# A merge's small products, their turning and its parts placed later among projections, and the last output half in a bank of its own

## The chip, the cores and the metric

The kernel runs on one core of one Trainium2 chip. The metric is the device time of one launch in microseconds (us), lower is better. Besides the plain runs there is one execution of the kernel before that the hardware profiler recorded, and all rows below are from it. The engines are named as the profile names them: PE is TensorE (matmul), DVE is VectorE, ACT is ScalarE, POOL is GpSimd, SP is SyncE, which issues most of the DMAs.

## The reference

One layer of a diffusion backbone on 1024 latent tokens (16 rows of 64) and 256 context tokens, model width 1024, all in fp32:

```python
# x: (1, 1024, 1024); modulated by adaLN, then one input projection for both branches
q, k, v, gate  = 8 heads of 64      # neighbourhood attention, window 8 x 16, plus all context keys
q, k, v, gate  = 4 heads of 128     # gated delta rule, chunks of 64, both directions
t_inv = triangular_solve(eye + a, eye)        # a: 64 x 64, strictly lower, one per chunk and direction
u = t_inv @ (v * beta);  w = t_inv @ (kb * exp(gc))
# scan over chunks from the context's final state
y = concat(attention * silu(gate), delta * silu(gate)) @ w_out
out = x + gate_ada * rmsnorm(y)
```

## The kernel before

Each fp32 product is made of three matmuls on split operands (hh·wh, hl·wh, hh·wl: a high and a low half). The program is written as Python generators; a scheduler orders the instructions of each engine from the program order, priorities and modelled times, and each engine then works through its own queue in that order.

The stage that the change touches is `phase_a2`. On PE it runs the projections for attention, pair of heads by pair (`self.fill`): the tiles pq, pk, pz of 512 columns (queries, keys and gate; pz2_0 and pz2_1 are the two 512-token halves of pair 2's gate), 24 matmuls each on 128x512. They accumulate in PSUM banks of one tag with three buffers ("pj"), so that a tile's first matmul waits until the tile three back has been read. `qk_out` reads a query or key tile twice: ACT copies out the high half (sh_), DVE subtracts to get the low half (sl_), both are stored to DRAM by SP. The sh_, sl_ and gate (st_z) tiles share four buffers.

Beside the projections two other generators are advanced by credits, per step of the fill 4 for `blocks()` and 1.5 for `merges()`. `blocks()` inverts the 32x32 diagonal blocks of the last group on DVE, some sixty short steps (ab_vv and tb_qh, L1255 and L1258, 80 partitions and 31 to 256 elements). `merges()` builds each head's 64x64 and 128-wide inverses out of these blocks, by `inv_merge`, which has parts in this order for a head h:

- l: load pmf (the products' other operand) and vl (the inverted blocks, four loads);
- t: on DVE three 32x32-wise transposes, vx from vl, vd from vx, ld from vd (lines 1291 to 1293), and ACT copies into tm;
- z: on PE the 32x32 products tz (two PSUM tiles of 20 products x 2), ACT copies them to zt, and ACT and POOL copy into xo and tm;
- u: on PE the 32x32 products tu, DVE copies them into tm and xo;
- w: on PE 64x64 products (tz2h_..., 20 of them), ACT copies them to z2;
- e: on PE 64x64 products (tu2h_...), DVE copies into tm, and SP stores tm to tm_dram.

tm is built in tm0 or tm1 (by the head's parity) and in tm2, which all heads share. The table MERGES ("0l 0t 1l 0z 1t 0u 0w 2l ...") gives the order in which the heads' parts are handed out, one by one.

Behind `phase_a2` come attention (scores sc from the loads kk, qh, ql) together with the delta scan, and last the output projection, whose tiles py are 512 columns wide. The last of them, (7, 1), is written in two halves of 256 columns, LAST = 256, one after the other into the same PSUM bank; `out_tile` then reads each half by ACT (sum of squares into ysq) and DVE (product with ggb).

## Time and profile before

| what | value |
|---|---|
| median of 3 runs | 851.81 us (849.72 to 855.88) |
| the profiled execution's own time | 848.82 us |
| its span | 847.1 us |
| PE busy | 814.2 us, 96% |
| DVE, ACT, POOL busy | 495.0, 418.0, 365.5 us |
| mean granted PE clock | 0.99 |
| longest PE wait | 5.58 us, head 0's first tz product, at 453.32 |

Between the profiled execution's time and its span lie 1.7 us. A busy share is an average over stages; what a stage waits for stands in its own rows. In a timeline row the first number is the start in us from the span's start, the second the length, and a bracket at the end holds the engine's idle time before the instruction and what ended it.

### The profile page before, as it was taken

The numbers are of one execution on the slowest core, as the hardware profiler recorded it, in microseconds if no ns is written. First come the engines' busy times: TensorE is split into PE (matmuls) and PEld (weight loads), VectorE is DVE, ScalarE is ACT, GpSimd is POOL, SyncE is SP. The second block draws the span as 40 slices with busy tenths as digits, with TensorE's granted clock in tenths as the row PEclk, the third lists the DMA queues.
The fourth block names the chain that finished last, engine by engine and source line by source line (L and its number), as shares of the span: only waits on it lengthen the run. The fifth ranks groups of instructions, "written<-read, shape, count | busy, mean of one in ns | idle before, by whom it ended". The sixth has DMA issues, their size and how long they took to land.

```text
span 847.1 us, 16613 instructions
## 1 busy us (share of the span) xinstructions
PE 814.2 (96%) x6170; PEld 695.3 (82%) x6170; DVE 495.0 (58%) x988; ACT 418.0 (49%) x1097; POOL 365.5 (43%) x436
## 2 busy tenths in 40 slices
PE   8999999999999999988997999899999999999996
PEld 6688887888788878878985787799898989878885
DVE  4673455546456757699926955556566565743342
ACT  4472525654564664643214334566666666753211
POOL 0042221363482572555452103565757567835121
PEclk9999999999999999999998999999999999999999
DMA  9986442254626626733688579996967923234261
GB/s 332 341 305 213 136 138 90 79 180 161 162 75 227 197 69 230 218 110 102 202 241 239 166 223 293 392 306 181 313 186 257 250 97 128 87 125 137 99 199 50
DMA packets 86343, 159.67 MB, mean 188 GB/s; under 512 B 18405, under 2 KB 45750, under 8 KB 84086
## 3 DMA queue, kind: packets, MB, share of 16 engines
q1 hardware_dynamic: 78774, 144.94, 54.0%
q10 hardware_dynamic: 7488, 13.67, 5.5%
q8 instruction: 49, 0.80, 0.4%
q14 instruction: 32, 0.26, 0.1%
HBM read 109.51 MB, written 52.42 MB: 191 GB/s over the span
## 4 chain that ended last, share of the span: by engine, by line
PE 76%; DMA 9%; DVE 7%; POOL 3%; issue 2%; ACT 2%; SPq 0%; DVEq 0%; POOLq 0%; ACTq 0%
PE py L1550 4%; PE py L1552 3%; PE py L1551 3%; PE pz L607 3%; PE pz L608 3%; PE pz L603 3%; PE pa L1437 3%; DMA vl<-yd 2%; PE po L942 2%; PE po L937 2%; PE tr L926 2%; PE sc L905 2%; PE pa L1422 2%; PE pv L618 2%; PE pv L617 2%; PE pv L616 2%
## 5 line engine op out<-in xcount | busy, mean ns | idle before, releaser
L909 DVE CUSTOM_DVE_ANT_0 pt<-sc,gm 128x544 f32<-128x544 f32 (+1 forms) x64 | 49.4, 772 | 32.3 <-PE sc L905 28.6
L910 ACT ACTIVATE pt<-pt,nm 128x544 f32<-128x544 f32 (+1 forms) x64 | 50.5, 789 | 31.1 <-DVE nm L909 30.7
L893 POOL TENSOR_TENSOR gm<-gt,mk 128x288 f32<-128x288 f32 (+1 forms) x48 | 46.5, 972 | 21.8 <-DVE nm L909 18.6
L1412 POOL TENSOR_SCALAR kd<-kt,kd 128x128 f32<-128x128 f32 x72 | 42.7, 604 | 18.7 <-PE pa L1451 18.2
L1040 DVE SCALAR_TENSOR_TENSOR acc_v<-xp_v,cols,acc_v 128x1282 f32<-128x1282 f32 x16 | 33.1, 2068 | 26.9 <-ACT acc_v L1038 26.6
L1193 POOL TENSOR_SCALAR_AFFINE_SELECT qe<-qe 128x256 f32<-128x256 f32 x32 | 29.0, 907 | 39.8 <-DVE qe L1192 39.8
L1616 DVE TENSOR_TENSOR finv<-py,ggb 128x512 f32<-128x512 f32 (+1 forms) x17 | 10.7, 656 | 51.4 <-ACT finv L1615 43.0
L603 PE MATMUL pz<-hh,wh_gz 128*128 128x512 f32 x96 | 38.9, 405 | 0.0
L607 PE MATMUL pz<-hl,wh_gz 128*128 128x512 f32 x96 | 38.8, 405 | 0.0
L608 PE MATMUL pz<-hh,wl_gz 128*128 128x512 f32 x96 | 38.8, 404 | 0.0
L1174 ACT ACTIVATE em<-em,gc 128x128 f32<-128x128 f32 x80 | 25.5, 390 | 25.7 <-DMA em<-gc_dram 22.9
L618 PE MATMUL pv<-wl_nv,hh 128*128 128x264 f32 x104 | 30.5, 296 | 4.8 <-DVE wl_nv L586 4.8
L1189 DVE SCALAR_TENSOR_TENSOR pm<-pk,nsc,em 128x128 f32<-128x128 f32 x80 | 23.5, 342 | 18.5 <-PE pk L1182 14.6
L1418 POOL TENSOR_SCALAR vb<-v,beta 128x128 f32<-128x128 f32 x40 | 24.2, 606 | 23.0 <-DVE y L1424 13.1
L586 POOL TENSOR_TENSOR wl_gz<-wr_gz,wh_gz 128x512 fp32r<-128x512 f32 x12 | 15.5, 1290 | 37.3 <-ACT wh_gz L585 35.8
L926 PE MATMUL tr<-c,pt 128*96 128x128 f32 (+1 forms) x192 | 31.4, 273 | 0.0
L1454 DVE SCALAR_TENSOR_TENSOR s<-s,egl,pa 128x128 f32<-128x128 f32 x64 | 19.4, 342 | 20.1 <-PE pa L1451 20.1
L924 ACT COPY tcx<-tc 128x256 f32<-128x256 f32 x64 | 23.5, 367 | 15.1 <-PE tc L919 14.5
L928 ACT COPY tl<-tr 96x384 f32<-96x384 f32 (+1 forms) x64 | 30.5, 476 | 0.0
L617 PE MATMUL pv<-wh_nv,hl 128*128 128x264 f32 x104 | 30.0, 291 | 0.0
L616 PE MATMUL pv<-wh_nv,hh 128*128 128x264 f32 x104 | 29.2, 292 | 0.0
L1615 ACT ACTIVATE finv<-py 128x512 f32<-128x512 f32 x14 | 8.3, 598 | 38.7 <-PE py L1552 20.5
(469 smaller groups left out, 2859.3 us busy)
## 6 DMA issues: line engine op xcount, KB each, us to landing
wada<-in_w_ada SPq DMA_DIRECT2D x16, 512.0 KB
em<-gc_dram SPq DMA_DIRECT2D x20, 256.0 KB
pm_dram<-pm SPq DMA_DIRECT2D x20, 256.0 KB
tm_dram<-tm SPq DMA_DIRECT2D x8, 640.0 KB
kk<-qk_dram SPq DMA_DIRECT2D x16, 320.0 KB
tm<-tm_dram SPq DMA_DIRECT2D x4, 1280.0 KB
kq_dram<-kq SPq DMA_DIRECT2D x4, 1152.0 KB
kq<-kq_dram SPq DMA_DIRECT2D x4, 1152.0 KB
```

The source lines that it names most:

```text
L603: r = nc.tensor.matmul(ps, wh, xh, start=(k == 0 and first), stop=False)
L607: nc.tensor.matmul(ps, wh, xl, start=False, stop=False)
L608: nc.tensor.matmul(ps, wl, xh, start=False, stop=(k == KC - 1))
L616: nc.tensor.matmul(ps, xh, wh, start=(k == 0), stop=False)
L617: nc.tensor.matmul(ps, xl, wh, start=False, stop=False)
L618: nc.tensor.matmul(ps, xh, wl, start=False, stop=(k == KC - 1))
L893: r = nc.gpsimd.tensor_tensor(self.gm[hh][:, 384 - n:384].rearrange("p (n c r) -> p n c r", c=nco, r=4), gv, self.mk[:, mo:mo + n].rearran ...
L909: nc.vector.tensor_tensor_reduce(pt[:, 384 - n:], sc[:, 512 - n:768], gm[:, 384 - n:], -1.0, 3.0e38, ALU.add, ALU.min, nm)
L910: self.last_exp = nc.scalar.activation(pt[:, 384 - n:], pt[:, 384 - n:], AF.Exp, bias=nm, scale=-1.0, accum_out=sums[:, ct, hh:hh + 1]).in ...
L926: self.pe(nc.tensor.transpose(pl[:m, rc * P:(rc + 1) * P], pt[:, 384 + (rc - 3) * m:384 + (rc - 2) * m], self.ident))
L1412: r = nc.gpsimd.tensor_scalar(kd[d], kt_[:, t, :], self.kd[:, h, d, t:t + 1], None, ALU.mult)
L1550: nc.tensor.matmul(py, mh[:, tt], wh[:, nn], start=(k == W_ORDER[0]), stop=False)
```

## The change

Three things are edited. `mm_chan` keeps the names of the last matmuls of its groups of three and `qk_out` that of the DVE instruction of the low half; with them, head 0's first transpose is ordered behind the last low half on DVE, and head 0's first tz product behind the last matmul recorded by then on PE (`order` sets an order on a queue, no semaphore). `merges()` holds head 0's part t until four steps of the fill are done and its part z until six, and its credit per step is 1.5 up to the sixth step and 2 from there. The second half of the last output tile gets a PSUM tile of its own, py7_2, and `out_tile` takes the halves from a list.

```diff
     def mm_chan(...):
-            nc.tensor.matmul(ps, wl, xh, start=False, stop=(k == KC - 1))
+            self.chans.append(nc.tensor.matmul(ps, wl, xh, start=False, stop=(k == KC - 1)).ins.name)
...
     def qk_out(...):
         if i:
-            nc.vector.tensor_tensor(kv(lo, "c r"), kv(src, "r c"), kv(hi, "c r").bitcast(F32), ALU.subtract)
+            r = nc.vector.tensor_tensor(kv(lo, "c r"), kv(src, "r c"), kv(hi, "c r").bitcast(F32), ALU.subtract)
         else:
-            nc.vector.scalar_tensor_tensor(lo, src, scale, hi.bitcast(F32), ALU.mult, ALU.subtract)
+            r = nc.vector.scalar_tensor_tensor(lo, src, scale, hi.bitcast(F32), ALU.mult, ALU.subtract)
+        self.low = r.ins.name
...
     def inv_merge(...):
-        nc.vector.transpose(vx, vl)
+        r = nc.vector.transpose(vx, vl)
+        if h == 0:
+            self.order(r, self.low)
...
-                    nc.tensor.matmul(pz[s2, t, :], pm[d][s1, t, s2], ld[s1, d, t, :], start=True, stop=True,
-                                     tile_position=(32 * b, 32 * b + 32))
+                    r = nc.tensor.matmul(pz[s2, t, :], pm[d][s1, t, s2], ld[s1, d, t, :], start=True, stop=True,
+                                         tile_position=(32 * b, 32 * b + 32))
+                    if h == d == t == b == 0:
+                        self.order(r, self.chans[-1])
...
     # output projection
-                for c0 in range(0, 512, LAST if tn == (7, 1) else 512):
-                    products(pys[tn], *tn, rest, c0, LAST if tn == (7, 1) else 512)
+                parts = [pys[tn]]
+                if tn == (7, 1):
+                    parts.append(ps.tile([P, 1024], F32, name="py7_2", tag="sc", bufs=1)[:, :512])
+                for i, py in enumerate(parts):
+                    products(py, *tn, rest, LAST * i, 512 // len(parts))
...
     def out_tile(...):
-            src = py[nn.start // 512][:, nn.start % 512:(nn.stop - 1) % 512 + 1]
+            src = py[i][:, nn.start % 512:(nn.stop - 1) % 512 + 1]
...
     def merges(parts):
+                while c == "0t" and steps < 4 or c == "0z" and steps < 6:
+                    yield
...
-        for _ in self.fill:
-            for i, r in enumerate((4, 1.5)):
+        for steps, _ in enumerate(self.fill, 1):
+            for i, r in enumerate((4, 1.5 if steps < 6 else 2)):
```

The lines of the rows below are moved by 1 to 5 in the changed kernel. First PE, in the middle of pair 2's gate, before: tz0_0 and tz0_1 are head 0's tz products.

```order
L603 MATMUL pz2_0_4738<-hh_115,wh_gz2_4_4733 128x512
L1305 MATMUL tz0_0_4491<-ld0_4338,pmf0_0_4330 32x32 [waits DMAHW4_49,DVE_49]
L1305 MATMUL tz0_0_4491<-ld0_4338,pmf0_0_4330 32x32 x19
L1305 MATMUL tz0_1_4514<-ld0_4338,pmf0_1_4332 32x32 [waits DMAHW5_49]
L1305 MATMUL tz0_1_4514<-ld0_4338,pmf0_1_4332 32x32 x19
L607 MATMUL pz2_0_4738<-hl_116,wh_gz2_4_4733 128x512
L608 MATMUL pz2_0_4738<-hh_115,wl_gz2_4_4734 128x512
L603 MATMUL pz2_0_4738<-hh_115,wh_gz2_4_4733 128x512
L607 MATMUL pz2_0_4738<-hl_116,wh_gz2_4_4733 128x512
L608 MATMUL pz2_0_4738<-hh_115,wl_gz2_4_4734 128x512
L603 MATMUL pz2_1_4797<-hh_115,wh_gz2_0_4727 128x512 [waits DVE_49]
```

The same engine in the changed kernel, the passage from pz2_0 to pz2_1, and then the end of pz2_1:

```order
L603 MATMUL pz2_0_4568<-hh_115,wh_gz2_4_4563 128x512
L607 MATMUL pz2_0_4568<-hl_116,wh_gz2_4_4563 128x512
L608 MATMUL pz2_0_4568<-hh_115,wl_gz2_4_4564 128x512
L603 MATMUL pz2_1_4660<-hh_115,wh_gz2_0_4557 128x512 [waits DVE_49]
L607 MATMUL pz2_1_4660<-hl_116,wh_gz2_0_4557 128x512
```

```order
L607 MATMUL pz2_1_4660<-hl_116,wh_gz2_4_4563 128x512
L1308 MATMUL tz0_0_4598<-ld0_4338,pmf0_0_4330 32x32 [waits DMAHW4_49,DVE_49]
L1308 MATMUL tz0_0_4598<-ld0_4338,pmf0_0_4330 32x32 x19
L1308 MATMUL tz0_1_4621<-ld0_4338,pmf0_1_4332 32x32 [waits DMAHW5_49]
L1308 MATMUL tz0_1_4621<-ld0_4338,pmf0_1_4332 32x32 x19
L608 MATMUL pz2_1_4660<-hh_115,wl_gz2_4_4564 128x512
```

The tz0 products moved from behind the nineteenth product of pz2_0 to ahead of the last one of pz2_1; the first product of pz2_1, with its wait on DVE, now comes ahead of them.

Second DVE at the same time, before: vx0, vd0, ld0 are head 0's transposes, sl_k20 is the low half of pair 2's first key tile.

```order
L1255 TENSOR_TENSOR tb2_qh0_4311<-ab_vv_4309 80x87 [waits DVE_49]
L1291 STREAM_TRANSPOSE vx0_4352<-vl0_4334 128x1024 [waits DMAHW5_49,DMAHW6_49,DMAHW4_49,DMAHW7_49,DMAHW1_49,DMAHW0_49]
L1258 TENSOR_TENSOR ab_vv_4309<-ab_vv_4309,tb2_qh0_4311 80x29x3 [waits DVE_49]
L1292 STREAM_TRANSPOSE vd0_4337<-vx0_4352 128x640 [waits DVE_49]
L1255 TENSOR_TENSOR tb2_qh0_4311<-ab_vv_4309 80x112 [waits DVE_49]
L1293 STREAM_TRANSPOSE ld0_4338<-vd0_4337 128x640 [waits DVE_49]
L1258 TENSOR_TENSOR ab_vv_4309<-ab_vv_4309,tb2_qh0_4311 80x28x4 [waits DVE_49]
L1255 TENSOR_TENSOR tb2_qh0_4311<-ab_vv_4309 80x135 [waits DVE_49]
L1291 STREAM_TRANSPOSE vx1_4545<-vl1_4335 128x1024 [waits DMAHW6_49,DMAHW7_49,DMAHW5_49,DMAHW4_49]
L1258 TENSOR_TENSOR ab_vv_4309<-ab_vv_4309,tb2_qh0_4311 80x27x5 [waits DVE_49]
L677 TENSOR_TENSOR sl_k20_4579<-pk2_0_4553,sh_k20_4578 128x512 [waits DMAHW0_49,Activation_49]
```

And in the changed kernel:

```order
L1256 TENSOR_TENSOR tb2_qh0_4311<-ab_vv_4309 80x207 [waits DVE_49]
L677 TENSOR_TENSOR sl_k20_4498<-pk2_0_4472,sh_k20_4497 128x512 [waits DMAHW0_49,Activation_49]
L1292 STREAM_TRANSPOSE vx0_4507<-vl0_4334 128x1024 [waits DMAHW6_49,DMAHW5_49,DMAHW7_49,DMAHW4_49,DMAHW1_49]
L1259 TENSOR_TENSOR ab_vv_4309<-ab_vv_4309,tb2_qh0_4311 80x23x9 [waits DVE_49]
L677 TENSOR_TENSOR sl_k21_4541<-pk2_1_4515,sh_k21_4540 128x512 [waits DMAHW2_49,Activation_49]
L1295 STREAM_TRANSPOSE vd0_4337<-vx0_4507 128x640 [waits DVE_49]
L1256 TENSOR_TENSOR tb2_qh0_4311<-ab_vv_4309 80x220 [waits DVE_49]
L1296 STREAM_TRANSPOSE ld0_4338<-vd0_4337 128x640 [waits DVE_49]
```

The transposes of head 0 moved behind sl_k20, and the steps of the inversion up to 207 elements moved ahead of both. SP's queue is the same in this place, from the loads of vl1 over the store of sl_q21 up to the store of sh_k20.

Third SP at the passage to attention, before: kk0_0 and kk0_1 are the keys for the first and second scores, z_dram the gate's stores, tm_dram1 and tm_dram2 the stores of heads 1 and 2. There tm_dram1's stores are twelve rows ahead of this piece.

```order
L681 DMA qk_dram_93<-sl_k31_5323 128x512 [waits DMAHW5_49,DVE_49]
L205 DMA kk0_0_5465<-qk_dram_93 64x1280 [waits DMAHW6_49,PE_49]
L205 DMA kk0_0_5465<-qk_dram_93 64x1280 [waits DMAHW7_49]
L705 DMA z_dram_95<-st_z30_5373 128x512 [waits DMAHW0_49,DVE_49]
L205 DMA kk0_1_5474<-qk_dram_93 64x1280 [waits DMAHW1_49,PE_49]
L205 DMA kk0_1_5474<-qk_dram_93 64x1280 [waits DMAHW2_49]
L705 DMA z_dram_95<-st_z31_5461 128x512 [waits DMAHW3_49,DVE_49]
L1351 DMA tm_dram2_87<-tm0_4336 128x1280 [waits DMAHW4_49,DVE_49]
```

And in the changed kernel:

```order
L682 DMA qk_dram_93<-sl_k31_5200 128x512 [waits DMAHW2_49,DVE_49]
L1273 DMA pmf3_1_5166<-pm_dram3_76 96x1280 [waits DMAHW3_49,PE_49]
L1356 DMA tm_dram1_86<-tm1_4339 128x1280 [waits DMAHW4_49,DVE_49]
L1356 DMA tm_dram1_86<-tm2_4340 128x1280 [waits DMAHW5_49,DVE_49,Pool_49]
L706 DMA z_dram_95<-st_z30_5365 128x512 [waits DMAHW6_49,DVE_49]
L205 DMA kk0_0_5465<-qk_dram_93 64x1280 [waits DMAHW7_49,PE_49]
L205 DMA kk0_0_5465<-qk_dram_93 64x1280 [waits DMAHW0_49]
L706 DMA z_dram_95<-st_z31_5431 128x512 [waits DMAHW1_49,DVE_49]
L205 DMA kk0_1_5474<-qk_dram_93 64x1280 [waits DMAHW2_49,PE_49]
L205 DMA kk0_1_5474<-qk_dram_93 64x1280 [waits DMAHW3_49]
L1356 DMA tm_dram2_87<-tm0_4336 128x1280 [waits DMAHW4_49,DVE_49]
```

The stores of head 1's tm moved to just ahead of the gate's first store, and kk0_1's loads from ahead of the gate's second store to behind it. On PE, head 2's products tz22 and tu22 moved at the same time from among pz3_0 and pz3_1 to behind the last product of pz3_1, next to the first scores.

More of the change, by code (lines that the diff above doesn't have):

```diff
@@ L194, in __init__ @@
         self.dbg = dbg or {}
-        self.na_first = None
+        self.na_first, self.chans = None, []
         self.gm = {}
@@ L1599, in phase4 @@
                 t, n = tn
-                for c0 in range(0, 512, LAST if tn == (7, 1) else 512):
-                    products(pys[tn], *tn, rest, c0, LAST if tn == (7, 1) else 512)
+                parts = [pys[tn]]
[3 more added lines that the diff above has]
+                    products(py, *tn, rest, LAST * i, 512 // len(parts))
                 if n:
-                    self.out_tile(p4, ps, t, [pys[t, n] for n in range(2)], ggb,
+                    self.out_tile(p4, ps, t, [pys[t, 0]] + parts, ggb,
                                   *xs[t % 2])
@@ L1658, in phase_a2 @@
         ended = [False, False]
-        first = True
+        first, steps = True, 0
         def advance(i):
```

## The prediction

> **What bounds the kernel now.** I read the busy shares first, then the waits of TensorE (PE), then the granted clock, and last the order of time around the longest wait.
>
> ```profile
> span 847.1 us, 16613 instructions
> PE 814.2 (96%) x6170; PEld 695.3 (82%) x6170; DVE 495.0 (58%) x988; ACT 418.0 (49%) x1097; POOL 365.5 (43%) x436
> engine line waited for: us in total, times, longest us
> PE tz L1305 <- DVE ld L1293: 5.6, 1, 5.6
> ...
> PE tz L1338 <- DVE tm L1329: 1.7, 2, 1.5
> ```
>
> PE is busy 96% of the span, so all the idle time of PE is about 33 us, and the change can win only from that or from the clock. The longest single wait is the one the change aims at: the first tz product of head 0 waits 5.6 us for ld. This is where it stands in PE's timeline (start, length, line, tile, count, and in brackets the idle time before it).
>
> ```profile
> 443.15 0.41 PE L603 MATMUL pz<-hh,wh_gz 128*128 128x512 f32 x1
> ...
> 447.35 0.40 PE L603 MATMUL pz<-hh,wh_gz 128*128 128x512 f32 x1
> 453.32 2.34 PE L1305 MATMUL tz<-ld,pmf 32*32 32x32 f32 x80 [5.58 <-DVE ld L1293]
> ...
> 457.89 0.63 PE L603 MATMUL pz<-hh,wh_gz 128*128 128x512 f32 x1
> 458.32 0.63 PE L607 MATMUL pz<-hl,wh_gz 128*128 128x512 f32 x1
> 458.74 0.46 PE L608 MATMUL pz<-hh,wl_gz 128*128 128x512 f32 x1
> 459.04 0.39 PE L603 MATMUL pz<-hh,wh_gz 128*128 128x512 f32 x1
> 459.27 0.39 PE L607 MATMUL pz<-hl,wh_gz 128*128 128x512 f32 x1
> ```
>
> From 443.15 to 447.35 lie 18 steps of the gate's products, 4.20 / 18 = 0.233 us each. After the wait the step is 0.43 us (457.89 to 458.32) until 458.74, then 0.23 again. The windows tell why (busy time of PE and PEld, then the rest; the number behind the engines is the granted clock, then the DMA share and GB/s).
>
> ```profile
> 450.00:452.00 2.00, 0.00 (x0) 0.00 (x0) 2.00 (x3) 0.00 (x0) 0.00 (x0) 1.00 0.90 225
> 452.00:454.00 2.00, 0.68 (x26) 0.68 (x28) 1.89 (x5) 1.52 (x4) 0.61 (x2) 0.51 0.65 205
> 456.00:458.00 2.00, 2.00 (x6) 1.52 (x6) 2.00 (x4) 1.36 (x3) 0.00 (x0) 0.50 1.03 358
> 458.00:460.00 2.00, 2.00 (x9) 1.58 (x8) 1.82 (x4) 1.97 (x6) 1.38 (x1) 0.79 0.86 262
> ```
>
> PE stops at 447.75, the clock is halved by about 452, and it comes back at about 458.7, some 5.4 us after PE restarted. In those 5.4 us about 45% of the work is lost, 2.4 us. So the place costs 5.58 + 2.4, 8 us, and that is the most that can be won here.
>
> [...] The rows above show 5.4 us, and the sum goes by them.
>
> **Part one: what PE meets once tz0 is out of the way.** In the new order PE finishes all 24 products of the gate's first half, pz2_0: five more at 0.233 behind 447.75, so it reaches pz2_1's first product at about 448.9. That product has a wait on VectorE (DVE) in both programs. It takes the PSUM bank of the keys' tile pk2_0, which sl_k20 (the keys' low half) must have read. Before, this wait never showed, since PE came there only at 457.89. So the question is when sl_k20 runs. DVE's timeline of before:
>
> ```profile
> 444.18 0.25 DVE L1255 TENSOR_TENSOR tb_qh<-ab_vv 80x87 f32<-80x87 f32 x1
> 449.82 1.25 DVE L1291 STREAM_TRANSPOSE vx<-vl 128x1024 f32<-128x1024 f32 x1 [5.39 <-DMA vl<-yd]
> 452.43 0.83 DVE L1293 STREAM_TRANSPOSE ld<-vd 128x640 f32<-128x640 f32 x1
> 455.06 1.25 DVE L1291 STREAM_TRANSPOSE vx<-vl 128x1024 f32<-128x1024 f32 x1 [1.13 <-DMA vl<-yd]
> 456.41 0.68 DVE L677 TENSOR_TENSOR sl_k<-pk,sh_k 128x512 fp32r<-128x512 f32 x1
> ```
>
> Now sl_k20 stands ahead of vx0. The 5.39 us in which DVE idled before vx0 are filled with twelve more short steps of the inversion (0.25 and somewhat more each as they grow, so some 4.2 us behind 444.4), and DVE gets to sl_k20 at about 448.6. But sl_k20 itself waits for more than DVE. It writes into one of four buffers that it shares with the halves before it, and the owner four back is sl_q21, whose store to DRAM must have landed. The same wait is in the trace once, one pair of tiles earlier, and it was long:
>
> ```profile
> 440.13 0.42 DVE L677 TENSOR_TENSOR sl_k<-pk,sh_k 128x256 fp32r<-128x256 f32 x1 [8.61 <-DMA qk_dram<-sl_q]
> ```
>
> When does sl_q21's store land? SyncE (SP) issues it behind the four loads of vl1, and the chain of waits has the last of those (start, length, what):
>
> ```profile
> 445.08 3.87 SPq L1285 DMA_DIRECT2D vl<-yd  x4
> 449.34 0.34 SPq L681 DMA_DIRECT2D qk_dram<-sl_q  x1
> 449.80 0.35 SPq L680 DMA_DIRECT2D qk_dram<-sh_k  x1
> 448.67 6.27 DMA vl<-yd
> 456.22 0.33 ACTq L582 DMA_DIRECT2D wr_nk<-in_w_in  x1
> ```
>
> The load lands at 448.67 + 6.27 = 454.94. The store was issued 0.67 later; with the same 6.27 it lands at 449.36 + 6.27 = 455.6. It must have landed by 456.41, when sl_k20 started; and the wr_nk load, which before waits for the keys' store issued right behind it (449.80), went at 456.22. SP's order is unchanged up to there, so the store lands when it did. Behind sl_k20 everything on DVE waits too, vx0 and the rest of the inversion, but the inversion has done more steps by then than before and is not late. Then sl_k20 ends at 455.7 + 0.68 = 456.4 and PE restarts at 456.5, not 453.32: **a wait of 7.6 us in place of 5.58.** PE is 3.2 us later, and has done five products (1.15) more: +2.0. The clock falls and returns as before, and the 5.4 slow us now hold 512-column products alone (12.6 of them at 0.43 instead of 0.233, 2.5 lost): +0.1 to 0.2. tz0 itself stands 23 products later, at about 464; vx0, vd0 and ld0 need at most 1.25 + 1.25 + 0.83, and sl_k21 and some short steps between them about 1.5, behind 456.4, so ld is there by about 461: no second wait. I take **+2.2**; the ends are +0.9 (the store lands as little as 5 us after its issue, at 454.4) and +2.9 (456.4).
>
> **Part two: the merge's parts are handed out later.** Most of them only trade places with projections. The place that I priced is the passage to attention. Head 2's last forty products (tz22, tu22) stood among the gate pz3's products; now they stand behind them, with only their own copies between. More telling is head 1: its tm stores (SP) and tu21 moved to the middle of pz3_0, so DVE's next copies into tm2 wait for that store. The low half of pz3_1's gate, its store, and behind this on SP the loads kk0_1 of the second scores are queued behind these copies. Before, kk0_1 was issued ahead of that store.
>
> ```profile
> 519.91 1.08 SPq L205 DMA_DIRECT2D kk<-qk_dram  x2
> 523.80 0.60 ACT L703 ACTIVATE st_z<-pz 128x512 f32<-128x512 f32 x1 [3.47 <-PE pz L608]
> 525.18 0.39 PE L902 MATMUL sc<-kk,qh 128*128 128x256 f32 x1 [0.52 <-DVE st_z L704]
> 526.10 6.57 DMA tm_dram<-tm
> 527.26 0.39 PE L902 MATMUL sc<-kk,qh 128*128 128x256 f32 x1
> 531.56 1.37 PE L1338 MATMUL tz<-xo,pmf 64*64 64x64 f32 x20
> 534.47 0.76 PE L1338 MATMUL tz<-tm,pmf 64*64 64x64 f32 x10 [1.54 <-DVE tm L1329]
> ```
>
> On before's clock (part one's shift left out): pz3_1 ended at 523.7; without about 2 us of head 2's products (1.37 for twenty tz, half as much for ten tu) it ends at 521.7, and pz3_0 some 6.8 earlier (24 x 0.233, and an estimated 1.2 for the 60 small products of tu2 between, since tz's 80 took 2.34 at half clock), at 514.9. The tm stores of head 1 then go out at about 515.5 and land 6.57 later, 522.1; three copies of 0.5 take DVE to 523.7, the gate's low half to 524.4, its store and kk0_1's issue to 525.2. The first scores come at about 525.5, hardly later. kk0_1 lands some 6.3 after its issue, 531.5, where PE wants it at 527.6: **a new wait of up to 4 us**. The wait of 1.54 at 534.47, a hand-over of the same tm2 by the next store, then goes under it. Net **+2.4**. Ends: nothing, if the loads land within 2 to 3 us of their issue (before, they had 7 us and the trace does not show when they came), and +5 if both transfers take what vl's first did, 9.09 us:
>
> ```profile
> 439.57 9.09 DMA vl<-yd
> ```
>
> **Part three: the last half tile in its own bank.** The end of the trace:
>
> ```profile
> 840.06 0.37 ACT L1615 ACTIVATE ysq<-py 128x256 f32<-128x256 f32 x1 [4.99 <-PE py L1552]
> 840.56 0.42 DVE L1616 TENSOR_TENSOR finv<-py,ggb 128x256 f32<-128x256 f32 x1 [4.77 <-ACT ysq L1615]
> 841.02 0.37 ACT L1615 ACTIVATE ysq<-py 128x256 f32<-128x256 f32 x1 [0.49 <-DVE finv L1616]
> ```
>
> ScalarE (ACT) squares the first half only when PE has finished both, then DVE, then ACT for the second half. With a bank of its own the first half is read while PE still multiplies the second, and the second ysq may start at 840.06 in place of 841.02: **-0.96**. The bank must be free at its first product; its last reader, an earlier output tile, is microseconds back. Bounds: 0 and -1.
>
> **The sum.** 2.2 + 2.4 - 0.96 = +3.6 on the profiled execution's 848.82 us: 852.4. The median of the runs is 2.99 above that execution, so it would be 855.4 on the median's scale. Two of three runs are within 3 us of the profiled one; I take 853.5.
>
> **Rivals.**
>
> *The store is early, and the change does what it says.* If sl_q21's store had landed by 449, sl_k20 runs when DVE reaches it, at 448.6 to 449.3, and PE waits about 0.5. Saved are 5.58 - 0.5, and the 2.4 of the clock, since PE never stops long enough: -7.5; with parts two and three -7.5 + 2.4 - 0.96 = -6.1, so 842.7 (845.7 on the median's scale). For it: no row shows this store's landing, only bounds. Against it: the 8.61 us wait of the same kind, and the load issued just ahead that took until 454.94. Chance 0.16.
>
> [...] In this trace vl0's, vl1's last landings follow the order of issue.
>
> *Slower: the passage to attention decides.* With 9.09 us for head 1's tm store as well as for kk0_1, part two gives its +5 and more: copies, gate half, store and loads are one chain, so both delays add, 2 x 2.5 on top of 2.4 less what PE still has to do. That is +7.4 + 2.2 - 0.96 = +8.6: 857.5 (860.4). It decides once a landing takes over 8 us there. For it: the DMA share of 0.98 to 1.09 around 510 to 540 that goes with such landings:
>
> ```profile
> 510.00:520.00 10.00, 9.96 (x89) 8.06 (x89) 5.79 (x12) 5.29 (x12) 1.79 (x4) 1.00 1.09 300
> ```
>
> Against it: 6.57 was measured in that very stretch. Chance 0.12.
>
> *A tie.* The store lands at about 453, so that sl_k20 releases PE as late as ld did, and kk0_1 comes in time: 0 + 0 - 0.96, 847.9 (850.8). Chance 0.10.
>
> **How the numbers follow.** Forecast 0.62, with the range that its bounds give: +0.9 + 0 - 1 to +2.9 + 5 - 0 is 848.7 to 856.7 on the profiled execution's scale and up to 859.7 on the median's. Low is 844, which takes in more than half of the first rival, high 859. One per cent (8.5 us) is about what a measurement of this kernel can tell from no change. Faster by more than that (below 843.3) needs the first rival in its better half: 0.07. Slower (above 860.3) needs the second in its worse half: 0.06. The rest, 0.87, is within 1%.
>
> **What would show it.** Step one is right if PE's longest wait is now that of a pz product for DVE's sl_k, 7 to 8 us, and DVE's sl_k row waits some 7 us for the store of sl_q; it is wrong if PE runs through from 443 to 465 at clock 1.00. Step two is right if the second scores wait for kk, and DVE's tm copies for tm_dram, near 520 to 535; wrong if sc has no wait above 1 us. Step three is right if the first ysq starts before PE's last product, and the second ysq 0.4 us behind it. The prediction as a whole would fail through a stage that I did not price, such as head 0's and head 2's hand-overs of tm2 between 470 and 510.

## The result and the profile after

The changed kernel takes 860.41 us (median of 19 runs, from 854.38 up) against 851.61 for the kernel before (19 runs beside it, 847.8 to 855.88). The ratio is 1.0095, 95% interval 1.0071 to 1.0119: slower by about 1%, where 853.5 was forecast and 859 was the upper end. One of the nineteen took 1594.86 us; medians here and below are of all runs, ratios leave out single executions far above the rest. The profiled execution took 854.90 us, 6.08 more than that of before.

The page's head and PE's longest waits after the change:

```profile
span 853.2 us, 16611 instructions
PE 819.9 (96%) x6170; PEld 700.0 (82%) x6170; DVE 496.6 (58%) x988; ACT 418.1 (49%) x1097; POOL 367.6 (43%) x436
PE pz L603 <- DVE sl_k L677: 6.8, 1, 6.8
...
PE sc L903 <- DMA kk<-qk_dram: 1.1, 1, 1.1
```

PE executes the same 6170 products and is busy 5.7 us longer with them. That is the first sign: the loss is not in waits, which add up to about the same (33 us of idle time before and after), but in products that ran slower.

The place of the first step, in the timelines of PE, DVE and SP after:

```profile
441.80 0.40 PE L603 MATMUL pz<-hh,wh_gz 128*128 128x512 f32 x1
447.16 0.40 PE L608 MATMUL pz<-hh,wl_gz 128*128 128x512 f32 x1
454.31 0.80 PE L603 MATMUL pz<-hh,wh_gz 128*128 128x512 f32 x1 [6.75 <-DVE sl_k L677]
461.63 1.45 PE L1308 MATMUL tz<-ld,pmf 32*32 32x32 f32 x80
...
446.38 0.37 DVE L1256 TENSOR_TENSOR tb_qh<-ab_vv 80x207 f32<-80x207 f32 x1
453.56 0.69 DVE L677 TENSOR_TENSOR sl_k<-pk,sh_k 128x512 fp32r<-128x512 f32 x1 [6.82 <-DMA qk_dram<-sl_q]
457.82 0.83 DVE L1296 STREAM_TRANSPOSE ld<-vd 128x640 f32<-128x640 f32 x1
...
446.79 0.34 SPq L682 DMA_DIRECT2D qk_dram<-sl_q  x1
```

PE waits 6.75 us for sl_k, and sl_k 6.82 us for the store of sl_q, which was issued at 446.79 and is there at 453.5. tz then finds ld ready.

The passage to attention. First PE, DVE and SP, then the windows with the granted clock:

```profile
518.91 1.38 PE L1343 MATMUL tz<-xo,pmf 64*64 64x64 f32 x20
520.12 1.15 PE L1343 MATMUL tz<-tm,pmf 64*64 64x64 f32 x17
525.51 0.38 PE L903 MATMUL sc<-kk,qh 128*128 128x256 f32 x1 [1.10 <-DMA kk<-qk_dram]
529.12 0.55 PE L903 MATMUL sc<-kk,qh 128*128 128x256 f32 x1
...
518.63 0.48 DVE L1334 COPY tm<-tu 32x320 f32<-32x320 f32 x1 [3.59 <-DMA tm_dram<-tm]
...
522.13 1.08 SPq L205 DMA_DIRECT2D kk<-qk_dram  x2
```

```profile
522.00:524.00 2.00, 1.55 (x26) 1.44 (x27) 1.33 (x3) 0.45 (x2) 2.00 (x3) 1.00 0.96 263
524.00:526.00 2.00, 0.90 (x12) 0.77 (x9) 0.51 (x2) 0.91 (x2) 0.37 (x1) 1.00 1.04 306
526.00:528.00 2.00, 2.00 (x77) 1.83 (x77) 0.73 (x2) 0.61 (x2) 0.75 (x1) 0.62 1.00 243
534.00:536.00 2.00, 2.00 (x9) 1.81 (x9) 1.88 (x4) 0.24 (x1) 1.00 (x3) 0.50 0.97 405
542.00:544.00 2.00, 2.00 (x23) 1.67 (x20) 0.12 (x2) 0.92 (x2) 0.07 (x1) 0.61 1.00 402
544.00:546.00 2.00, 2.00 (x31) 1.57 (x30) 0.31 (x1) 1.21 (x3) 0.00 (x0) 1.00 1.00 414
```

The hand-over of tm2 is there (DVE waits 3.59 us for the tm store), the first scores wait 1.10 us for kk, and the second scores at 529.12 wait for nothing. But the clock falls to 0.50 at 526.5 and stays there to 544.0, with PE busy nearly all the time. In the profiled execution of before it did not fall there at all.

The end, ACT's two squares and PE's last product (the row of before, for the distance, first):

```profile
839.68 0.28 PE L1552 MATMUL py<-wl,mh 128*128 128x256 f32 x1
```

```profile
844.26 0.37 ACT L1623 ACTIVATE ysq<-py 128x256 f32<-128x256 f32 x1 [2.15 <-PE py L1557]
847.10 0.37 ACT L1623 ACTIVATE ysq<-py 128x256 f32<-128x256 f32 x1 [2.37 <-PE py L1557]
...
846.72 0.28 PE L1557 MATMUL py<-wl,mh 128*128 128x256 f32 x1
```

From PE's last product to the end of the span it was 847.1 - 839.68 = 7.42 us, and is 853.2 - 846.72 = 6.48: 0.94 saved.

So the 6.08 us can be laid out along the program, by the starts of rows that both traces have. The first product of pair 3's queries, the landmark in the middle, is this row before and after:

```profile
465.51 0.40 PE L603 MATMUL pq<-hh,wh_nq 128*128 128x512 f32 x1
```

```profile
463.35 0.40 PE L603 MATMUL pq<-hh,wh_nq 128*128 128x512 f32 x1
```

| stretch | before | after | difference |
|---|---|---|---|
| start to pz2_0's first product | 443.15 | 441.80 | -1.35 (nothing changed here: scatter between executions) |
| to pq3_0's first, tu0 counted in (1.50 after) | 22.36 | 23.05 | +0.69 |
| to the first scores | 59.67 | 60.66 | +0.99 |
| first scores to PE's last product | 314.50 | 321.21 | +6.71 |
| to the end of the span | 7.42 | 6.48 | -0.94 |

The sum is +6.10. Nearly all of the loss stands behind the first scores, where the forecast had about 2 us.

### The profile page after: what moved, and what is told of

Its sections match the earlier page's. It is cut to its first block, busy times and chain, and to the rows that moved or that the text cites. A ratio compares the mean times of both kernels' runs of the same rounds, so it can differ in the third digit from the quotient of the medians.

```text
span 853.2 us, 16611 instructions
## 1 busy us (share of the span) xinstructions
PE 819.9 (96%) x6170; PEld 700.0 (82%) x6170; DVE 496.6 (58%) x988; ACT 418.1 (49%) x1097; POOL 367.6 (43%) x436
## 4 chain that ended last, share of the span: by engine, by line
PE 74%; DVE 9%; DMA 9%; ACT 3%; issue 2%; POOL 2%; SPq 1%; ACTq 0%; DVEq 0%; POOLq 0%
PE py L1555 4%; PE py L1557 3%; PE py L1556 3%; PE pz L607 3%; PE pz L608 3%; PE pz L603 3%; PE pa L1442 2%; PE po L943 2%; PE tr L927 2%; PE sc L906 2%; PE po L938 2%; PE pv L618 2%; PE pv L617 2%; PE pv L616 2%; PE sc L903 2%
## 5 line engine op out<-in xcount | busy, mean ns | idle before, releaser
L603 PEld LDWEIGHTS pz<-hh,wh_gz 128*128 128x128 f32 x96 | 18.6, 193 | 11.2 <-DVE sl_k L677 7.2
```

The costliest lines, as they stand in the source:

```text
L603: r = nc.tensor.matmul(ps, wh, xh, start=(k == 0 and first), stop=False)
```

## The experiments

Theory after the result, called the clock theory: the passage of small products and short waits ahead of the first scores lets the clock fall to one half, and attention's first products, small too, keep it there for 17 us and more. Rival, the DMA theory: what was moved later (stores, hand-overs, loads) holds attention up, and the clock only goes along. "Half clock" below is the time below 0.97 by windows of half a us; the stretch of 7 to 7.5 us around 452 to 459 is in the kernel before as well, and so are shorter ones between 318 and 391 us and one at the very end.

**The changed kernel again.**

> The changed kernel once more, beside the others on one chip. Its nineteen runs lie in two groups, 854.4 to 858.5 us at a mean granted clock near 0.981 and 860.4 to 866.2 us near 0.968. Clock theory: most of the loss arises behind the first scores, where TensorE drops to half clock at about 526 us, and the two groups differ in how long that half clock lasts; a profile of the upper group would show it beyond 543 us. DMA theory: the loads and hand-overs that were moved later hold attention up, the clock only follows; the groups would then differ in waits for DMAs, not in the length of the half clock.

858.07 us (12 runs, 853.72 to 862.81), ratio 1.0081 (1.0052 to 1.0110). The profiled execution came from the upper group, 861.66 us at a mean clock of 0.973:

```profile
530.00:535.00 5.00, 5.00 (x138) 4.19 (x136) 1.42 (x4) 3.29 (x9) 1.67 (x4) 0.50 1.04 412
550.00:555.00 5.00, 5.00 (x25) 3.89 (x24) 1.98 (x5) 1.55 (x4) 1.58 (x3) 0.50 1.02 420
555.00:560.00 5.00, 5.00 (x42) 4.58 (x42) 1.95 (x6) 1.83 (x5) 2.60 (x4) 0.76 1.04 371
```

Here the half clock lasts from 526.5 to 557.5, 31 us, against 17.5 in the first profile. The stretch from the first scores to PE's last product, in the kernel before, in the first profile of the changed kernel and in this one:

```profile
525.18:839.68 314.50, 307.45 (x2672) 271.19 (x2672) 168.60 (x453) 172.21 (x505) 171.59 (x230) 1.00 0.61 192
525.51:846.72 321.21, 314.98 (x2672) 277.63 (x2672) 168.36 (x452) 172.51 (x506) 170.05 (x228) 0.97 0.61 189
526.75:853.47 326.72, 320.79 (x2672) 282.70 (x2672) 168.52 (x452) 172.73 (x506) 170.24 (x228) 0.95 0.60 185
```

With the same 2672 products PE is busy 7.53 us longer in the first profile and 13.34 in this one. Counted with the clock of each window, the half clock there is 17.05 and 30.72 us long: 0.44 and 0.43 us lost per us at half clock. PE's idle time in the stretch falls by 0.82 us in the first profile, so 7.53 - 0.82 is the 6.71 of the table.

The mean clock of an execution that was not profiled gives an estimate of its whole time at half clock, 2 x (1 - clock) x span: 17, 32 and 46 us for the three profiled ones, where the windows add up to 16, 33 and 46. By that the 35 executions of the kernel before beside this run spent 13 to 38 us at half clock, median 22, and these twelve of the changed kernel 32 to 55, median 34. So the kernel before loses the clock too, only less often or for less long, and its profiled execution is one of the better ones.

**The bank alone.** The kernel before with `py7_2` and the list in `out_tile`:

```diff
-                for c0 in range(0, 512, LAST if tn == (7, 1) else 512):
-                    products(pys[tn], *tn, rest, c0, LAST if tn == (7, 1) else 512)
+                parts = [pys[tn]]
+                if tn == (7, 1):
+                    parts.append(ps.tile([P, 1024], F32, name="py7_2", tag="sc", bufs=1)[:, :512])
+                for i, py in enumerate(parts):
+                    products(py, *tn, rest, LAST * i, 512 // len(parts))
```

> The kernel before with the last output half in its own bank and nothing else. Both theories: the second square starts some 0.4 us behind the last product in place of 1.3 us, 0.96 us saved, all else as before: ratio 0.998 to 1.000, in one group of runs.

848.20 us, ratio 0.9983 (0.9953 to 1.0013). The size fits, the interval takes in no change; the trace shows it better (the second square starts 0.4 us behind the last product, as above). Two of its twelve runs, 853.96 and 855.45, have a mean clock of 0.98 instead of 0.99, as some of the kernel before have.

**Without the two orders.**

```diff
-        if h == 0:
-            self.order(r, self.low)
...
-                    if h == d == t == b == 0:
-                        self.order(r, self.chans[-1])
```

> The changed kernel without its two orders (head 0's transpose behind the keys' low half, head 0's first product behind the recorded matmul); the held parts, the larger credit and the bank stay. Queue order: head 0's products stand again among pz2_0, and head 2's tz22 between pz3_0 and pz3_1. My step one: the wait for ld of 5.6 us is back, that for sl_k gone, about 2 us gained against the changed kernel. Clock theory: the thin passage ahead of the first scores is broken up by eight to sixteen gate products, so the half clock from 526 us goes and with it another 5 to 7 us: 847 to 851. DMA theory: the stores and loads at the passage are still later than before, so the loss behind the first scores stays: 853 to 856.

856.54 us, ratio 1.0053 (1.0022 to 1.0084). The median is just above the range of the DMA theory, but the runs are in two groups: four from 848.58 to 851.72 with a mean clock of 0.987 to 0.990, in or near the clock theory's range, and eight from 854.42 to 859.90 with 0.976 to 0.981. The profiled execution belongs to the lower one (850.73), has the wait for ld again (4.3 us) and none for sl_k. Its one stretch of half clock here, 511.0 to 514.5, is not at the passage but ahead of it, behind head 1's small tu products and their wait for tm:

```profile
509.06 0.18 PE L1325 MATMUL tu<-zt,vd 32*32 32x32 f32 x1 [2.31 <-DVE tm L1350]
511.00:514.50 3.50, 3.50 (x10) 2.71 (x9) 2.24 (x5) 1.82 (x4) 0.00 (x0) 0.52 1.03 338
516.00:528.00 12.00, 11.73 (x110) 9.54 (x108) 3.19 (x6) 3.86 (x9) 3.25 (x7) 1.00 0.59 158
```

At the passage itself, here from tz22 at 516.2 to the first scores at 527.8, gate products stand among head 2's small ones and the clock holds at 1.00, as the clock theory has it. Where the eight slower runs lose the clock was not profiled.

**Added full-size products.** In `inv_merge`, for head 2, behind tz22 and behind each half of tu22:

```diff
+            for k in range(n):   # n = 4, three times
+                r = nc.tensor.matmul(pd, self.lastw[k % KC], self.hh[:, k % KC, 0:512], start=(k == 0), stop=(k == n - 1))
+                self.order(r, last)
+                last = r.ins.name
```

> The changed kernel with twelve added full-size products (128x512, into a spare bank, read by nobody): four behind tz22, four and four behind the halves of tu22, ahead of the first scores. They cost 12 x 0.233 = 2.8 us at most, less what they fill of the waits of 1.1, 0.3 and 0.3 us there. No load, store or hand-over is moved earlier. Clock theory: TensorE stays busy enough, no half clock from 526 to 543 us, 4 to 5 us faster than the changed kernel in its lower group. DMA theory: 1 to 3 us slower.

851.09 us, ratio 1.0018 (0.9986 to 1.0050). Twelve products more, and 7 us less than the changed kernel on the same chip; the wait for sl_k (7.2 us) and SP's order are as there. The rows of PE and the windows of the profiled execution:

```profile
522.92 1.19 PE L1351 MATMUL pd<-hh,wh_gz 128*128 128x512 f32 x4
525.17 1.19 PE L1351 MATMUL pd<-hh,wh_gz 128*128 128x512 f32 x4
527.42 1.20 PE L1351 MATMUL pd<-hh,wh_gz 128*128 128x512 f32 x4
529.42 0.38 PE L904 MATMUL sc<-kk,qh 128*128 128x256 f32 x1
...
525.00:530.00 5.00, 5.00 (x85) 3.88 (x82) 1.83 (x4) 1.48 (x4) 0.13 (x1) 1.00 1.01 295
530.00:535.00 5.00, 4.80 (x176) 4.05 (x175) 3.57 (x9) 3.04 (x8) 2.32 (x4) 1.00 1.04 350
```

The clock holds at 1.00 with the DMA share where it was (1.01 and 1.04). The first scores come 3.9 us later than in the changed kernel and the program still ends 5.4 us earlier (847.8 against 853.2). The DMA theory falls with this run: no transfer was made earlier (the loads of kk are issued 1.5 us later than in the changed kernel). Two of the twelve runs (864.88 and 866.32, mean clocks 0.972 and 0.975, in the median but not in the ratio) show that the cure isn't sure.

**The store ahead of the loads.**

```diff
+            if h == 1:
+                self.order(r, self.qlow)      # r: each load of vl1; qlow: the store of sl_q21
```

> The changed kernel, with one order more on SP's queue: the four loads of vl1 behind the store of sl_q21, which before this stood behind them. Step one says that sl_k20 waits for that store and PE for sl_k20; then the store lands some 6 us after an earlier issue, the wait of 6.8 to 7.6 us shrinks to about 3 or less, or vanishes, and with it the 2.4 us of half clock at 452 to 459. The passage to attention stays as in the changed kernel, so the half clock from 526 us stays. Expected 6 to 9 us below the changed kernel: 849 to 852. If the wait for sl_k were another's (ACT, DVE's queue), it stays at 7 us and the time at 857.

860.10 us, ratio 1.0133 (1.0086 to 1.0179): not faster, against the expectation.

```profile
443.56 0.34 SPq L682 DMA_DIRECT2D qk_dram<-sl_q  x1
...
452.64 0.69 DVE L677 TENSOR_TENSOR sl_k<-pk,sh_k 128x512 fp32r<-128x512 f32 x1 [7.05 <-DMA qk_dram<-sl_q]
...
441.00 11.35 DMA pmf<-pm_dram
```

The store was issued 3.2 us earlier than in the changed kernel and, by sl_k's start, landed 0.9 us earlier (452.64 against 453.56), 9.0 us behind its issue; PE's own wait for sl_k became 5.8 us in place of 6.75. The loads of pmf, issued at 441.00, landed at 452.35, and sl_k, which waits for the store, started at 452.64. So the place behind vl1 was not what held the store. No row shows the store's own landing; whether the store waited for pmf's loads is not shown. The half clock lasted from 523.0 to 557.5 in this execution, which sets its time.

**Both cures.** The last two edits together.

> Both cures at once: vl1's loads behind the store of sl_q21, and twelve added full-size products among head 2's last products (work that nobody reads). If the two losses are independent, both are gone: 7 us below the filler alone, 842 to 845. If one half clock only makes room for the other (a fixed budget of the throttle), about 850.

853.09 us, ratio 1.0022 (0.9990 to 1.0054): no faster than the filler alone, so neither expectation came true. PE's wait for sl_k is 5.5 us in its profile against 7.2 with the filler alone, a gain too small to show in the times. The profiled execution (847.97) has no half clock behind 458 until its last 3 us.

**The filler on a quarter of the array.**

```diff
-                r = nc.tensor.matmul(pd, self.lastw[k % KC], self.hh[:, k % KC, 0:512], ...)
+                r = nc.tensor.matmul(pd[A], self.lastw[k % KC][A, 0:64], self.hh[A, k % KC, 0:512], ..., tile_position=(0, 0))
```

> The filler once more, at the same twelve places and with as many columns (512), but on a quarter of the array: 64 rows by 64 columns of weights. PE is as busy in time as with the full-size filler. If the clock falls because PE waits there, it holds as well: 851, no half clock behind 526 us. If it falls because little of the array works, the half clock comes back in most executions: 856 to 860.

858.37 us, ratio 1.0082 (1.0048 to 1.0115): as slow as without any filler.

```profile
524.31 1.96 PE L1351 MATMUL pd<-hh,wh_gz 64*64 64x512 f32 x4
...
535.00:540.00 5.00, 5.00 (x134) 4.42 (x128) 2.14 (x5) 2.51 (x6) 2.33 (x4) 0.50 1.03 341
545.00:550.00 5.00, 5.00 (x37) 4.53 (x37) 0.83 (x2) 2.72 (x7) 2.14 (x4) 0.50 1.01 419
```

As many columns at the same places, PE busy without a gap, and the clock stays at 0.50 to 554. The profiled execution is one of the slowest (862.67; the runs go from 848.21 up), and its half clock had begun at 523, just ahead of the filler and behind a wait of 1.17 us for xo: in this execution these products, the last of them started at 532.00, did not end the half clock. That they do not keep the clock up either is shown by the runs: nine of the twelve with the full-size filler have a mean clock of 0.986 or more, two of these twelve, and none of the changed kernel's twelve. PE's busy time does not tell the two fillers apart: from 525 to 530 it was 5.00 of 5 us with both, at a clock of 1.00 with the products on 128 x 128 and of 0.50 with those on 64 x 64.

**A credit of 3.**

```diff
-            for i, r in enumerate((4, 1.5 if steps < 6 else 2)):
+            for i, r in enumerate((4, 1.5 if steps < 6 else 3)):
```

> The changed kernel with a credit of 3 instead of 2 per step behind the sixth: the merges' parts are handed out sooner, six of pz3_1's products stand again between tz22 and tu22, and kk0_1's loads on SP come ahead of the gate's second store. Step one's wait stays. Clock theory: fewer thin products in a row ahead of the first scores, the half clock is rarer or shorter: 850 to 855, between the changed kernel and the one with the filler. If six products aren't enough, 857 as before.

866.40 us, ratio 1.0190 (1.0137 to 1.0243): the slowest kernel here, against the expectation. Handing out sooner made new waits (tu for tm 3.8 us in two places) and three more stretches of half clock, 487.0 to 494.5, 514.5 to 521.5 and 538.5 to 566.0.

**Products in the first gap too.** The filler at the passage, no order on the transposes, and thirty products of 320 columns between pz2_0 and tz0:

```diff
+            if j == 2 and gr == 0:
+                for k in range(30):
+                    r = nc.tensor.matmul(pd, self.hh[:, k % KC, 0:P], self.hh[:, k % KC, 0:320], start=(k == 0), stop=(k == 29))
+                    self.order(r, self.chans[-1])
+                    self.chans.append(r.ins.name)
```

> The changed kernel without the transposes' order on DVE (so that ld comes before sl_k20 again), with thirty added products of 320 columns between pz2_0 and tz0, where PE waits, and the twelve full-size ones at the passage; the added ones are read by nobody. Thirty at an estimated 0.233 x 320 / 512 = 0.146 us are 4.4 us, in a wait of about that length. Clock theory: idle time alone halves the clock at 452 us, so with the gap filled the clock stays at 1.00 there too, 2.4 us come back, and with no drop at the passage: 844 to 848, below the kernel before. If the drop at 452 us has another cause, the half clock from 452 to 459 stays, 848 to 851.

858.69 us, ratio 1.0125 (1.0087 to 1.0163): slower, against both expectations. PE has two waits behind the filled gap, and one more later:

```profile
449.74 4.56 PE L707 MATMUL pdw<-hh 128*128 128x320 f32 x30
454.77 1.45 PE L1314 MATMUL tz<-ld,pmf 32*32 32x32 f32 x80 [0.47 <-DVE ld L1302]
458.49 0.80 PE L603 MATMUL pz<-hh,wh_gz 128*128 128x512 f32 x1 [2.26 <-DVE sl_k L678]
```

The filled gap kept the clock through 455, but tz's 80 small products and the wait of 2.26 us behind them came next, and it fell at 457.5, for 7.5 us. It fell again at 474.5 in a wait of 3.6 us for xo that the changed kernel's profile does not have. This filler only moved the gap and gained nothing.

**Without the transposes' order.** Only the first two lines of the diff of "without the two orders" are taken out.

> The changed kernel without one of its two orders: head 0's transposes stand ahead of sl_k20 again, while tz0 stays behind all of pz2_0. Step one says that the wait of 7 us for sl_k becomes one for ld that ends at about 453, 4.4 us long, and that pz2_1 then waits little. About 2 us less than the changed kernel at that place. At the passage tz22 and tu22 again stand apart from each other, with twenty gate products between, but some stand behind the first scores: by the clock theory drops are rarer than in the changed kernel, 849 to 856; by the DMA theory 854 to 857.

865.32 us, ratio 1.0201 (1.0162 to 1.0240). The first place went as step one says: tz waits 2.7 us for ld, then pz 1.9 us for sl_k, 4.6 in place of 6.8 to 7.6. The passage went worse: the scores wait 2.8 us for kk, and the clock is at one half from 530 to 561. The expectation for the whole time was missed by either theory; the long half clock is that of the slowest executions of the others.

**Full-size products after the drop.** Sixteen behind tu3, ahead of tz23:

```diff
+        if h == 3:
+            for k in range(16):
+                r = nc.tensor.matmul(pd, self.hh[:, k % KC, 0:P], self.hh[:, k % KC, 0:512], start=(k == 0), stop=(k == 15))
+                self.order(r, late)
+                late = r.ins.name
```

> The changed kernel with sixteen added full-size products (128x512, read by nobody) behind the first scores and tu3, ahead of tz23, that is after the half clock has begun. At half clock they take 16 x 0.43 = 6.8 us, two of the 3.4 to 3.5 us steps of which all half-clock stretches so far are multiples. Clock theory: the half clock begins at 526 us as before and ends with these products, at about 534 to 540, in every execution, in place of 544 or 557; the cost of the products (some 5 us) and the clock won back about cancel, 853 to 858, without the upper group. Rival (a half clock lasts as long as it will, the later attention's work decides): it lasts to 544 or 557 plus the products' time, 861 to 868.

861.25 us, ratio 1.0130 (1.0092 to 1.0169), so the time is the rival's; the clock is not. This execution was 7 us behind the first profile already where the passage begins (tz22 at 525.86 in place of 518.91). Of these, 4.2 us were there at pq3_0's first product (467.57 in place of 463.35): this execution, unlike the first profile, has a half clock near its start, 15.5 to 26.0. The rest came with an idle time of 1.86 us ahead of tu, which the profile puts down to no engine, and a stretch of half clock of its own, 520.5 to 524.5.

```profile
540.43 5.83 PE L1341 MATMUL pd<-hh 128*128 128x512 f32 x16
...
542.00:544.00 2.00, 2.00 (x6) 1.53 (x5) 0.20 (x2) 0.00 (x0) 1.88 (x6) 0.50 0.00 0
544.00:546.00 2.00, 2.00 (x9) 1.50 (x7) 0.62 (x2) 0.00 (x0) 2.00 (x3) 0.87 0.00 0
546.00:548.00 2.00, 2.00 (x33) 1.80 (x31) 0.00 (x0) 0.81 (x2) 0.89 (x1) 1.00 0.42 77
```

The half clock, begun at 530.5, ends at 545.0, some 4 us into the sixteen products and before the last of them. Three of the four runs lie within 0.5 us of each other (861.02 to 861.43), where the changed kernel's twelve scatter over 9; four runs are few. The full-size products ended the half clock of this execution; what ends it in the others, where it returns among attention's own products, isn't shown.

**Four products only.** The first four of the twelve.

> The filler cut down to its first four full-size products (between tz22 and tu22, 0.9 us). If the first wait of the passage starts the half clock, four do what twelve did: 849 to 851, 1.9 us of added work less. If the whole passage of small products counts, the half clock comes back in a part of the executions: 851 to 858.

858.82 us, ratio 1.0110 (1.0070 to 1.0149): no help. The half clock is there from 526.5 to 544.0, to the half us as in the first profile of the changed kernel. So it isn't the wait between tz22 and tu22 alone that starts it. Whether the small products behind it count, or the wait of 1.0 us ahead of the first scores, this run doesn't tell apart.

The half-clock stretches behind 460 us of all profiled executions, beside their times (the last 1 to 4.5 us, at half clock in every one, left out):

| kernel | us | half clock behind 460 |
|---|---|---|
| before | 848.82 | none |
| changed | 854.90 | 17.5 |
| changed again | 861.66 | 31 |
| bank alone | 848.18 | 3.5 |
| no orders | 850.73 | 3.5 |
| filler | 849.47 | none |
| store first | 859.05 | 34.5 |
| both cures | 847.97 | none |
| quarter filler | 862.67 | 2 (from 451.5), 31 |
| credit 3 | 869.33 | 7.5, 7, 27.5 |
| first gap filled | 858.97 | 5 (from 457.5), 7.5, 4 |
| no transpose order | 863.99 | 3.5, 31 |
| late filler | 864.80 | 3 (from 455.5), 4, 14.5 |
| four products | 856.68 | 17.5, 3.5 |

## Why the prediction was wrong

**Step one, the wait for sl_k: right in its mechanism, too dear.** The wait of 5.58 us went, and one of 6.75 us for sl_k came in its place, which waits 6.82 us for the store of sl_q: the chain as forecast, with 7.6 us. The store landed 6.7 us behind its issue, where 6.3 was taken, but SP issued it earlier against PE's place, 4.99 us behind pz2_0's first product (446.79 and 441.80), before 6.19 us (449.34 and 443.15). The stretch costs +0.69, not +2.2. The second error in it is "the clock falls and returns as before" with the same 5.4 slow us behind the restart: the clock returned at 458.2, 3.9 us behind PE's restart at 454.31. Its whole length is what was the same: 6.83 and 6.82 us, with each window counted by its clock.

The moments at which the clock falls and returns show why. In the first profile they are 379.70, 386.54, 451.38, 458.21, 526.48 and 543.54, read from windows of a quarter us: 0, 2, 21, 23, 43 and 48 steps of 3.413 us behind the first. In the profile of before they are 318.91, 322.33, 383.77, 387.18, 452.03 and 458.86, at 0, 1, 19, 20, 39 and 41 such steps. The windows of half a us between 440 and 600 in the profiles of the quarter filler, credit 3, the first gap filled, no transpose order, the late filler and the four products have such a grid too, each its own. Behind both kernels' long wait the clock returned at the end of the first step that holds full-size products almost throughout (455.4 to 458.9 before, with PE restarted at 453.32; 454.8 to 458.2 after, restarted at 454.31); with the late filler it was the first step that lies wholly in the sixteen, 541.1 to 544.5.

**Step two, the passage: the step that failed.** The links were there: DVE's copies wait for head 1's tm store (3.59 us), kk0_1 is issued behind them, and the 1.54 us wait of before is gone. Their times were off. Set on before's clock (0.66 us later, by the first two rows of the table), the second tm store went out at 510.8 and not at 515.5, took 8.5 us and not 6.57, and kk0_1 was issued at 522.8 and not at 525.2. The price of +2.4 was put on a wait of the second scores for kk. That wait did not come: the second scores came at 529.12 with no wait, 7.0 us behind the issue of kk0_1. What came was a wait of 1.10 us for kk0_0, +0.99 in its stretch, and behind the first scores +6.71 that stood in no term: 17.5 us at half clock, and 31 in an execution of the upper group. I had read the clock at 452 to 459 and costed it at 2.4 us, and put the clock at the passage at nothing without a reason, although the change put eighty 64x64 products (by the trace's rows) with three waits (0.32, 0.27 and 1.10 us) between the last gate product and the first scores, and tz's eighty 32x32 ones right behind these. The filler shows that this passage is the cause (7 us back with more work to do), the quarter filler that as many products on 64 x 64 of the array do not do what those on 128 x 128 did (858.37 us against 851.09); in the late filler's one profile the half clock ended 4.1 us into full-size work.

No wait ahead of the drop at 526.5 is longer than 1.10 us; the work ahead of it is on 64 x 64 of the array, but for the four products of the first scores, and tz's on 32 x 32 had just begun. The half clock stayed with PE busy 17.29 of the 17.5 us from 526.5 to 544.0, and 5.00 of 5 us from 530 to 535 in the second profile.

**Step three, the bank: right.** 0.94 us against 0.96.

**The rivals.** The early store did not happen: it went out at 446.79, and sl_k started at 453.56. The slower one had the right size (857.5 to 860.4) for a wrong reason: both transfers would have had to take 9 us; the tm store took 8.5 (issued at 510.15, waited for until 518.63) and kk0_1 less than 7.0 (kk0_0 took 4.65, the chain's row "520.82 4.65 DMA kk<-qk_dram"). The DMA share that spoke for it was not 0.98 to 1.09 throughout: from 520 to 530 it was 0.89. The chance of 0.06 for slower by over 1% was too small, since every path to it went through waits. The scale was a minor error: the profiled execution of before, at 848.82, is 2.8 us below its median of 19 runs, and that of the changed kernel is from its lower group, 5.5 below. That one per cent is about what can be told from no change was too cautious: the interval of the result is 0.24% to either side.

What stays open: why the half clock lasts five steps in one execution and nine in the next of the same program. Both fell at nearly the same moment, 526.5 and 526.7, with the first scores 1.2 us later in the second; no run here sets where the grid lies against the work. Open too is whether the small products or the waits between them start a half clock, whether the rows or the columns of the array count (the quarter filler halves both), and where the slower executions of the kernel before lose theirs. No kernel of the study beats the kernel before beyond the measurement; the bank alone comes nearest (0.9983).

## What to carry to other kernels

Ask of every stretch that a change makes thinner whether the clock holds there, not only what it waits for: here a row of small-tile products with short gaps costs 1.7 us in the list of waits and 7.5 us in the clock. PE's total busy time at an equal number of products is the quick test, the granted clock by windows the sure one: with the bank alone PE was busy 3.0 us longer than before in an execution that was 0.6 us faster. When small products must be moved, leave full-size ones between them; here twelve, 3.6 us in all, held the clock in most runs (a mean of 0.986 or more in nine of twelve), and four, 1.2 us, did not (0.972 to 0.981 in six). A wait that is taken away from in front of a queue is worth only what the next wait in that queue leaves of it: here 5.58 us went and 6.75 came.

## What the hardware showed that I had not expected

- The half clock outlasted the waits ahead of it. In the first profile PE idled some 1.7 us ahead of it, in waits of 0.32, 0.27 and 1.10 us; it then lasted 17.5 us, in others up to 34.5, with PE busy nearly throughout (17.29 of the 17.5 us).
- Twelve products on 64 x 64 of the array, 512 columns each, did not hold the clock up (mean clock 0.986 or more in two of twelve runs); as many on 128 x 128 did in nine of twelve, and in one profile with sixteen of these in a row a half clock ended 4.1 us after their start.
- Within each of eight executions the falls and returns of the clock lie on one grid of 3.41 us, and each us at half clock cost 0.44 and 0.43 us of PE's time in the two profiles where it was worked out.
- Issuing a store 3.2 us earlier (443.56 in place of 446.79) let sl_k, which waits for it, start 0.9 us earlier (452.64 in place of 453.56).
